# Attention blocks, scans and output stores given out later in a hybrid two-layer encoder, weight splits put first, one copy moved into the unit before

## The chip, the cores and the metric

The kernel runs on one core of a Trainium2 chip. The metric is the device time of one execution in microseconds; the median of three runs of the kernel before is 2544.51 us. The core has TensorE (PE in the profile, its weight loads apart as PEld), VectorE (DVE), ScalarE (ACT), GpSimd (POOL) and SyncE (SP, which here only issues DMAs). Each engine takes its own instructions in the order of the program and waits on semaphores for the others.

## The reference

Two layers run over 640 tokens: 512 of a prompt and 8 times 16 of a decode batch with 512 cached keys each. A layer computes, in float32:

```
h = rms_norm(x);  z = h @ w_in            # u, v | q, k, v, indexer | q, k, v | three gates
oa = u * (block-causal W_s @ rms_norm(gelu(v)) + bias)              # branch a
ob = softmax attention, 8 query heads on 2 kv heads, keys chosen by
     the top 128 (132) of an indexer's relu scores                   # branch b
oc = stick-breaking attention, 8 heads: w = exp(log_sigmoid(z) + suffix sum of log_sigmoid(-z))
x += (sum of sigmoid(gate_i) * (o_i @ w_br_i)) @ w_out
x += (silu(g) * up) @ w_ffn_out
x += sigmoid(rms_norm(x) @ w_ple_gate) * (p @ w_ple_proj)
```

The new keys and values of both attentions, the indexer keys and the normalised v rows are outputs as well.

## The kernel before

The 640 tokens lie on the free axis as two halves of 320 (`HN`), the 1024 model columns as 8 tiles of 128 partitions. All projections are fp32 work done as three single-pass products: weights and activations are split into a high and a low part, and `rows` (three matmuls of 320 columns for each k tile, PSUM tile `pd`) sums high x high, low x high and high x low. `token_tiles` does the same with tokens as the stationary side (`pn`). Attention uses the names `cz`, `czs` (branch c logits, prompt and decode), `bl`, `bls` (branch b), `ix`, `ixs`, `is` (indexer), `tpw` (transposes of the weights of a block), `av`, `avs`, `avb` (weights times values), `hcs`, `sp` (sums for the head norms and their spread).

Weights come in chunks of at most 128x1024 in a fixed order (`CHUNKS`). `load_chunk` issues the DMA into one of two `raw` tiles, copies it into one of three `hi` tiles on ACT (L219) and subtracts on DVE, or on POOL for the chunks 18 to 36 of a layer, into one of three `lo` tiles (L220). A layer is a list of units in the order of the string `ORDER`, then the merges of the branches, the output projection, the feed-forward part and the last gate. The units named cq, ck (branch c queries, keys), bq, bk, av, au and ga are projections of one 128-column tile each, 48 matmuls, 7 us.

Attention is written as Python generators that are put between the projection matmuls. `add` queues a task in one of two lists (`sc` for branch c, `si` for the indexer and branch b) with a due time `self.T + START`; `mm` advances the clock `T` by an assumed price for each matmul; `pump`, called every six matmuls or so, runs every task that is due up to its next `yield`, whose value is the time to wait (a multiple of `LAG`). `logits_room` holds the one double PSUM tile `qk` of the logits for a given time, `room` the two `tp` tiles. `until` runs tasks to their end before a unit that needs them. After that a scheduler settles each engine's own order from these priorities.

The pieces that the change and the prediction touch are these. `stick_prompt` (branch c, one block of 128 queries) makes the logits, adds the mask on DVE (L952), takes a sigmoid on ACT (L955), scans on DVE (L942), subtracts (L959) and hands over to `av_prompt`, which transposes, multiplies by the values, copies to the tile `ots` (L937) and stores it (L938). `dsa_prompt` is the same for branch b, with the softmax in lines 1032 to 1040. `stack_q` makes the split query tiles `qs` (copy on ACT L549, subtraction on POOL L550), `stack_k` the key tiles `ks` and `kl` (L560 to L563). `u_bk` projects branch b's keys; `key_norm`, called in the following unit bq0, spreads their norm with a POOL copy `hrb` (L616) and ten matmuls `sp`. `head_rms` makes `hcs`, for which ACT first squares the tile (`hsq`, L607).

Of the kernel before, what the change touches and what calls it, by code (L numbers as in the profile page):

```python
# [9 lines left out]
F32 = mybir.dt.float32  # L10
F32R = mybir.dt.float32r
BF = mybir.dt.bfloat16
U32 = mybir.dt.uint32
AF = mybir.ActivationFunctionType
OP = mybir.AluOpType
# [43 lines left out]
def _chunk(w, ks, cols):  # L59
# [4 lines left out]
ORDER = ("cq0 ck0 av0 cq1 av1 ck1 cq2 au0 au1 ck2 cq3 au2 ck3 au3 "  # L64
         "bk0 bq0 ga0 ga1 bq1 ga2 bq2 ga3 ga4 bq3 ga5 ga6 ga7")

# [78 lines left out]

ND, NQ, NTP = 4, 1, 2
LAG, LOAD1, LOAD4, START = 1.2, 3.5, 8.0, 2.5
PAIRED = (("c", 0), ("c", 1), ("c", 2), ("c", 3), ("b", 0), ("b", 1), ("b", 2), ("b", 3), "bs")
# [22 lines left out]
class Net:  # L171
    def __init__(self, tc, A, cst, big, wp, wk, sm, ps):
        nc = tc.nc
        self.tc, self.nc, self.A = tc, nc, A
        self.cst, self.big, self.wp, self.wk, self.sm, self.ps = cst, big, wp, wk, sm, ps
        self.con = con = cst.tile([128, C_N], F32, name="con")
        self.ident = con[:, C_ID:C_ID + 128]
        self.cmask = con[:, C_CM:C_CM + 128]
        self.adm = con[:, C_ADM:C_ADM + 128]
        self.gcol = []  # L180
        for l in range(L):
            g = cst.tile([128, G_N], F32, name=f"gcol{l}")
            (nc.gpsimd if l else nc.sync).dma_start(g, A["cols"][l])
            self.gcol.append(g)
        self.ones = cst.tile([128, 1], F32, name="ones")
        nc.vector.memset(self.ones, 1.0)
        self.zero = cst.tile([128, 1], F32, name="zero")
        nc.vector.memset(self.zero, 0.0)
        self.half = cst.tile([128, 16], F32, name="half")
        nc.vector.memset(self.half, -0.5)  # L190
        self.T, self.qk_free, self.tp_due = 0.0, 0.0, [0.0, 0.0]
        self.n_loaded = 0
        self.ready = []
        self.later = []
        self.x = big.tile([128, KD, NT], F32, tag="m20", name="x0")
        self.load_chunk(3, lambda k: nc.sync.dma_start(self.x[:, k], A["xT"][:, k]))
        nc.sync.dma_start(con, A["con"])
        for k in range(3, KD):
            if k in (3, 6):
                self.load_chunk()  # L200
            nc.sync.dma_start(self.x[:, k], A["xT"][:, k])


    def load_chunk(self, pieces=1, also=None):
        nc, i = self.nc, self.n_loaded
        self.n_loaded += 1
        w = CHW[i % NCH] // pieces
        raw = self.wp.tile([128, 1024], F32, tag="raw", name=f"raw{i}", bufs=2)
        hi = self.wp.tile([128, 1024], F32R, tag="hi", name=f"hi{i}")
        lo = self.wp.tile([128, 1024], F32R, tag="lo", name=f"lo{i}")  # L210
        low = nc.gpsimd if LO_POOL[0] <= i % NCH < LO_POOL[1] else nc.vector
        for p in range(pieces):
            c = slice(w * p, w * p + w)
            nc.sync.dma_start(raw[:, c], self.A["w"][i // NCH, i % NCH, :, c])
            if also:
                also(p)

            def split(c=c):
                nc.scalar.activation(hi[:, c], raw[:, c], AF.Copy)  # L219
                low.tensor_tensor(lo[:, c], raw[:, c], hi[:, c].bitcast(F32), op=OP.subtract)  # L220

            if p:
                self.later.append(split)
            else:
                split()
        self.ready.append((hi, lo))
# [56 lines left out]
    def tp(self, name):  # L283
        self.tp_due = [self.tp_due[1], self.T + 1.0]
        return self.ps.tile([128, 512], F32, tag="tp", name=name, bufs=NTP)
# [97 lines left out]
    def batch_rows(self, b):  # L383
        t = self.at.tile([128, 8, 16], BF, tag="es", name="es", bufs=1)
        nc, con = self.nc, self.con
# [4 lines left out]
    def pump(self):  # L390

        if self.busy:
            return
        self.busy = True
        for q in (self.sc, self.si):
# [10 lines left out]
    def step(self, q, t):  # L406
# [9 lines left out]
        t.past |= t.held  # L416
        t.due = self.T + (wait[0] if t.held else wait)

    def until(self, q, *names):
# [181 lines left out]
    def u_bk(self, j, ch):  # L601
        nc, S = self.nc, self.S
# [6 lines left out]
        self.head_rms(sq, r, 64)  # L609
        S["bkz"], S["rk"] = z, r  # L610

    def key_norm(self):
        nc, S, l, gl = self.nc, self.S, self.l, self.gl
        z, r = S["bkz"], S["rk"]
        rb = self.wk.tile([128, 5, 2, 64], F32, tag="t2", name="hrb", bufs=1)
        nc.gpsimd.tensor_copy(rb.rearrange("p t s d -> p (t s) d"),  # L616
                              r.rearrange("p t s -> p (t s)")[:, :, None].to_broadcast([128, 10, 64]))
        b0, b1 = self.spread(lambda t: rb[:, t].rearrange("p s d -> p (s d)"))
# [39 lines left out]
    def reload(self, br):  # L658

        src = []  # L660
        for j in range(4):
            if br == "a":
                t = self.S["au"][:, j]
# [130 lines left out]
    def index_prompt(self):  # L794
# [17 lines left out]
        for i in range(1, 4):  # L812
# [14 lines left out]
            for hp in range(4):  # L827
                yield from self.logits_room(LAG * (0.4 + 1.7e-3 * n))
                qk = self.qk2("ix")
# [19 lines left out]
        iws = self.at.tile([128, 2, 128], F32, tag="iws", name="iws", bufs=1)  # L849
        ia = self.at.tile([128, 8, 16], F32, tag="osb", name="iwa", bufs=1)  # L850
        nc.vector.tensor_tensor(ia, iw[:, 4][:, :, None].to_broadcast([128, 8, 16]),
# [18 lines left out]
    def index_sample(self):  # L870
# [5 lines left out]
        for b in range(NB):  # L876
            nc.gpsimd.tensor_copy(kx[:, PAST:], ikr[:, 16 * b:16 * b + 16])
            yield 0.4
            yield from self.logits_room(LAG * 0.9)
            qk = self.qk2("ixs")  # L880
# [12 lines left out]
            else:  # L893
                yield LAG * 0.9
                for hf in range(2):
                    p = self.tp("is")
# [28 lines left out]
    def av_prompt(self, w, vt, o, j, i, m):  # L925
# [4 lines left out]
        yield from self.room(1)  # L930
        ot = self.at.tile([128, 128], F32, tag="os" + m, name="ots", bufs=1)
        av = self.tp("av")
# [4 lines left out]
        nc.vector.tensor_copy(ot, av[:, :128])  # L937
        nc.sync.dma_start(o[:, j, 128 * i:128 * i + 128], ot)  # L938

# [4 lines left out]
    def stick_prompt(self, j, i, q, k, vt):  # L944
# [14 lines left out]
        nc.vector.tensor_tensor(g[:, :, :n], g[:, :, 1:n + 1], g[:, :, :n], op=OP.subtract)  # L959
        yield (LAG * (0.6 + 6.6e-3 * n),)  # L960
        yield from self.av_prompt(g, vt, self.A["s_oc"][self.l], j, i, "c")

    def stick_sample(self):
# [7 lines left out]
        for b in range(NB):  # L971
# [4 lines left out]
            yield 0.6  # L976
            yield from self.logits_room(LAG * 1.2)
            qk = self.qk2("czs")
# [24 lines left out]
            if b < NB - 1:  # L1003
                kc = [self.past("kc", self.A["c_k"][l, b + 1, :, j]) for j in range(4)]
                loaded = self.T + LOAD4
            at = self.at.tile([128, 128], F32, tag="osc", name="at", bufs=1)
            nc.scalar.activation(at, av[:, :128], AF.Copy)
# [13 lines left out]
    def dsa_prompt(self, j, i, q):  # L1021
        nc, S = self.nc, self.S
        vt, k, rq = S["bvp"], S["bk"], S["rq"]
        n = 128 * (i + 1)
        yield from self.logits_room(LAG * (0.4 + 4.2e-3 * n))
        qk = self.qk2("bl")
# [17 lines left out]
    def dsa_sample(self):  # L1044
# [10 lines left out]
        def first():  # L1055
            ra = self.at.tile([128, 2, 4, 16], F32, tag="osb", name="ra", bufs=1)
            for s in range(2):
# [150 lines left out]
```

## Time and profile before

| what | us |
|---|---|
| median of three runs | 2544.51 |
| lowest, highest | 2542.89, 2545.09 |
| the profiled execution's own time | 2545.36 |
| its span from the first to the last instruction | 2543.6 |
| TensorE busy in the span | 2469.8 (97%) |
| weight loads busy | 2347.1 (92%) |
| DVE, ACT, POOL busy | 1356.2 (53%), 940.9 (37%), 316.8 (12%) |

The busy time of an engine is the time in which one of its instructions runs; matmuls are pipelined, so one that starts every 0.147 us is shown with 0.31 us. PEclk is the clock that TensorE was granted as a share of full speed. Windows are given in us from the start of the span. A wait row names the instruction that waited, what it waited for, the us in total, the number of times and the longest. Layer one runs up to about 1270, layer two after it; attention lies in the first 500 us of each.

### The profile page before, as it was taken

The page shows a single profiled execution, that of the slowest core. Times are in us where ns is not written, and L with a number is a line of the kernel's source. Part 1 is how long each engine was busy: PE and PEld are TensorE (multiplying, and loading weights), DVE is VectorE, ACT ScalarE, POOL GpSimd, SP SyncE. Part 2 cuts the span into 40 slices and gives each one's busy share as a digit, 9 for nine tenths or more (in the row PEclk, how much of TensorE's full clock was granted, in tenths as well). Part 3 has the DMA queues.
Part 4 walks back from the last instruction along what each step waited for, and adds up shares of the span by engine and source line. Part 5 has one row for each costly group of instructions (what it writes and reads, how often), then busy time and mean ns, then how long its engine had stood idle before and what let it go on. Part 6 is the DMA issues. An engine that isn't in the chain of part 4 may idle for free.

```text
span 2543.6 us, 42312 instructions
## 1 busy us (share of the span) xinstructions
PE 2469.8 (97%) x17528; PEld 2347.1 (92%) x17528; DVE 1356.2 (53%) x2447; ACT 940.9 (37%) x1365; POOL 316.8 (12%) x375
## 2 busy tenths in 40 slices
PE   8989999999999999999999998999999999999999
PEld 8887778899999999999998877788999999999999
DVE  5885754554544334345558948446445443343454
ACT  4644554532332122123346345556223321221231
POOL 1122322100001000000011223221000000010100
PEclk9999999999999999999999999999999999999999
DMA  5222244532422222222342221445323222222222
GB/s 192 86 68 85 73 128 143 157 105 75 133 69 75 75 75 76 76 74 78 101 142 87 72 82 65 140 130 178 99 75 127 69 81 76 75 74 77 69 81 75
DMA packets 102399, 242.89 MB, mean 95 GB/s; under 512 B 11152, under 2 KB 33952, under 8 KB 102208
## 3 DMA queue, kind: packets, MB, share of 16 engines
q1 hardware_dynamic: 99552, 229.81, 29.1%
q0 software_dynamic: 2656, 10.38, 1.1%
q8 instruction: 138, 2.26, 0.4%
q14 instruction: 53, 0.43, 0.1%
HBM read 221.07 MB, written 19.08 MB: 94 GB/s over the span
## 4 chain that ended last, share of the span: by engine, by line
PE 84%; DVE 8%; issue 3%; ACT 2%; POOL 2%; DMA 1%; SPq 0%; DVEq 0%; POOLq 0%; ACTq 0%
PE pd L273 71%; PE pn L273 4%; DVE cg L942 2%; PE tpw L281 2%; PE av L273 1%; DVE m L788 1%; DVE sc L791 1%; PE bl L273 1%; POOL qs L550 1%; PE czs L273 1%; ACT hi L219 1%; PE ixs L273 1%; PE bls L273 1%; DVE cg L959 1%; PE is L273 1%
## 5 line engine op out<-in xcount | busy, mean ns | idle before, releaser
L219 ACT ACTIVATE hi<-raw 128x1024 fp32r<-128x1024 f32 (+4 forms) x306 | 316.5, 1034 | 1114.1 <-PE pd L273 656.4
L273 PE MATMUL pd<-fh,lo 128*128 128x320 f32 x1664 | 513.5, 309 | 0.0
L273 PE MATMUL pd<-fh,hi 128*128 128x320 f32 x1664 | 513.4, 309 | 0.0
L273 PE MATMUL pd<-fl,hi 128*128 128x320 f32 x1664 | 513.1, 308 | 0.0
L273 PE MATMUL pd<-xh,hi 128*128 128x320 f32 x1568 | 498.4, 319 | 0.0
L273 PE MATMUL pd<-xh,lo 128*128 128x320 f32 x1568 | 492.1, 314 | 2.4 <-DVE lo L220 2.4
L273 PE MATMUL pd<-xl,hi 128*128 128x320 f32 x1568 | 493.9, 315 | 0.0
L220 DVE TENSOR_TENSOR lo<-raw,hi 128x1024 fp32r<-128x1024 f32 (+4 forms) x268 | 368.1, 1373 | 143.6 <-ACT hi L219 143.0
L273 PEld LDWEIGHTS pd<-xh,hi 128*128 128x128 f32 x1568 | 298.0, 190 | 17.9 <-issue 16.8
L273 PEld LDWEIGHTS pd<-fh,hi 128*128 128x128 f32 x1664 | 312.3, 188 | 0.1
L273 PEld LDWEIGHTS pd<-fh,lo 128*128 128x128 f32 x1664 | 312.3, 188 | 0.0
L273 PEld LDWEIGHTS pd<-fl,hi 128*128 128x128 f32 x1664 | 312.3, 188 | 0.0
L273 PE MATMUL pd<-mid,hi 128*128 128x320 f32 x1408 | 309.9, 308 | 0.0
L273 PEld LDWEIGHTS pd<-xh,lo 128*128 128x128 f32 x1568 | 299.1, 191 | 9.6 <-issue 6.5
L273 PEld LDWEIGHTS pd<-xl,hi 128*128 128x128 f32 x1568 | 299.0, 191 | 4.8 <-issue 4.3
L273 PEld LDWEIGHTS pd<-mid,hi 128*128 128x128 f32 x1408 | 235.5, 188 | 0.0
L273 PE MATMUL pd<-mid,lo 128*128 128x320 f32 x704 | 217.0, 308 | 0.0
L749 POOL TENSOR_TENSOR fu<-fu,fg 128x640 f32<-128x640 f32 x44 | 68.9, 1566 | 772.3 <-DVE fu L337 772.3
L730 DVE TENSOR_TENSOR x<-x,pd 128x320 f32<-128x320 f32 x128 | 61.7, 486 | 193.4 <-PE pd L273 191.6
L337 DVE TENSOR_TENSOR fu<-pd,rs 128x320 f32<-128x320 f32 x88 | 43.3, 492 | 191.9 <-PE pd L273 191.9
L273 PEld LDWEIGHTS pd<-mid,lo 128*128 128x128 f32 x704 | 132.1, 188 | 0.0
L337 DVE TENSOR_TENSOR gt<-pd,rs 128x320 f32<-128x320 f32 x96 | 46.9, 490 | 156.7 <-PE pd L273 156.6
(264 smaller groups left out, 3765.5 us busy)
## 6 DMA issues: line engine op xcount, KB each, us to landing
raw<-w SPq DMA_DIRECT2D x270, 512.0 KB, 3.6
kc<-c_k SPq DMA_DIRECT2D x64, 256.0 KB, 5.3
kc<-c_v SPq DMA_DIRECT2D x64, 256.0 KB, 3.7
raw<-w SPq DMA_DIRECT2D x16, 384.0 KB, 3.1
raw<-w SPq DMA_DIRECT2D x11, 468.0 KB, 4.2
ka<-b_k SPq DMA_DIRECT2D x16, 256.0 KB, 2.8
kv<-b_v SPq DMA_DIRECT2D x16, 256.0 KB, 3.0
x<-xT SPq DMA_DIRECT2D x8, 320.0 KB, 5.8
```

What stands on the lines that cost most here:

```text
L219: nc.scalar.activation(hi[:, c], raw[:, c], AF.Copy)
L220: low.tensor_tensor(lo[:, c], raw[:, c], hi[:, c].bitcast(F32), op=OP.subtract)
L273: self.nc.tensor.matmul(out, a, b, start=start, stop=stop)
L281: self.nc.tensor.transpose(out, src, self.ident)
L337: self.nc.vector.tensor_tensor(dst[:, sl], pt[h][:, :HN], self.rs[:, sl], op=OP.mult)
L550: nc.gpsimd.tensor_tensor(q[b, s], z[a, :NP], q[a, s].bitcast(F32), op=OP.subtract)
L730: self.nc.vector.tensor_tensor(x[:, c, sl], x[:, c, sl], pt[h][:, :HN], op=OP.add)
L749: nc.gpsimd.tensor_tensor(u, u, g, op=OP.mult)
L788: nc.vector.max(out=m8, in_=sc[:, :n])
L791: nc.vector.match_replace(out=sc[:, :n], in_to_replace=m8, in_values=sc[:, :n], imm_value=TAKEN)
L942: self.nc.vector.tensor_tensor_scan(r, r, self.zero.to_broadcast([128, n]), 1.0, op0=OP.mult, op1=OP.add)
L959: nc.vector.tensor_tensor(g[:, :, :n], g[:, :, 1:n + 1], g[:, :, :n], op=OP.subtract)
```

## The change

`ORDER` moves the unit bq1 to directly behind bq0 and the later ones of branch b one place earlier. New attention tasks become due 6.0 instead of 2.5 after they are queued (`START`). The waits between the scan and the transposes of a branch c block, and the holds of the logits tile, are longer by 0.5 to 1.0 times `LAG`; a `tp` tile counts as taken for 1.5 instead of 1.0, and the indexer's `is` step now asks for both. The store of `ots` is issued 2.0 later, through a list that `pump` empties (`soon`, `catch_up`). The small tiles `ots`, `at`, `iwa`, `ra` and `es`, each alone or in pairs under a tag with one buffer, share the tag `os` with three. The two instructions of a weight split are traced with a priority raised by 200. The copy `hrb` moves from `key_norm` (unit bq0) to the end of `u_bk`. No instruction of TensorE, DVE or POOL is added or removed; ACT has four table loads fewer in the program.

```
-         "bk0 bq0 ga0 ga1 bq1 ga2 bq2 ga3 ga4 bq3 ga5 ga6 ga7")
+         "bk0 bq0 bq1 ga0 ga1 bq2 ga2 ga3 bq3 ga4 ga5 ga6 ga7")
...
-ND, NQ, NTP = 4, 1, 2
-LAG, LOAD1, LOAD4, START = 1.2, 3.5, 8.0, 2.5
+ND, NQ, NTP, OS = 4, 1, 2, 3
+LAG, LOAD1, LOAD4, START = 1.2, 3.5, 8.0, 6.0
...
-                nc.scalar.activation(hi[:, c], raw[:, c], AF.Copy)
-                low.tensor_tensor(lo[:, c], raw[:, c], hi[:, c].bitcast(F32), op=OP.subtract)
+                with self.tc.high_priority(offset=200):
+                    nc.scalar.activation(hi[:, c], raw[:, c], AF.Copy)
+                    low.tensor_tensor(lo[:, c], raw[:, c], hi[:, c].bitcast(F32), op=OP.subtract)
...
-        self.tp_due = [self.tp_due[1], self.T + 1.0]
+        self.tp_due = [self.tp_due[1], self.T + 1.5]
...
+    def soon(self, delay, f):
+        self.todo.append((self.T + delay, f))
+    def catch_up(self, all=False):
+        while self.todo and (all or self.todo[0][0] <= self.T):
+            self.todo.pop(0)[1]()
...
+        rb = self.wk.tile([128, 5, 2, 64], F32, tag="t2", name="hrb", bufs=1)
+        nc.gpsimd.tensor_copy(rb.rearrange("p t s d -> p (t s) d"),
+                              r.rearrange("p t s -> p (t s)")[:, :, None].to_broadcast([128, 10, 64]))
+        S["bkz"], S["rkb"] = z, rb
...
-        ot = self.at.tile([128, 128], F32, tag="os" + m, name="ots", bufs=1)
+        ot = self.at.tile([128, 128], F32, tag="os", name="ots", bufs=OS)
...
-        nc.sync.dma_start(o[:, j, 128 * i:128 * i + 128], ot)
+        self.soon(2.0, lambda: nc.sync.dma_start(o[:, j, 128 * i:128 * i + 128], ot))
...
-        yield (LAG * (0.6 + 6.6e-3 * n),)
+        yield (LAG * (1.6 + 6.6e-3 * n),)
...
-        yield from self.logits_room(LAG * (0.4 + 4.2e-3 * n))
+        yield from self.logits_room(LAG * (1.2 + 4.2e-3 * n))
```

The first place is TensorE behind the unit bq3 of layer one, where the logits `bl` of that unit's first block are made from `qs`. Before:

```order
L273 MATMUL avs<-kc,wT 32x128 [waits DMAHW1_49]
L273 MATMUL avs<-kc,wT 32x128 x3
L273 MATMUL bl<-ks,qs 128x256 [waits Pool_49]
L273 MATMUL bl<-kl,qs 128x256
L273 MATMUL pd<-xh,hi_4194 128x320
L273 MATMUL bl<-ks,qs 128x256 [waits Pool_49]
L273 MATMUL bl<-kl,qs 128x256
```

In the changed program the same logits stand in one piece:

```order
L274 MATMUL avs<-kc,wT 32x128 [waits DMAHW0_49]
L274 MATMUL avs<-kc,wT 32x128 x3
L274 MATMUL bl<-ks,qs 128x256 [waits Pool_49]
L274 MATMUL bl<-kl,qs 128x256
L274 MATMUL bl<-ks,qs 128x256 [waits Pool_49]
L274 MATMUL bl<-kl,qs 128x256
L274 MATMUL pd<-xh,hi_3932 128x320
```

Between the last matmul of bq3 and the first of these rows stand 12 projection matmuls in the order before and 36 in the changed one.

The second place is ACT in layer one, where branch c's first key tiles `ks` and `kl` are made beside the indexer's `ixr` and the weight split of the next chunk (`hi_950` before, `hi_929` now). Before:

```order
L833 ACTIVATE ixr<-ix 128x2x384 [waits PE_49,Pool_49]
L833 ACTIVATE ixr<-ix 128x2x384 [waits DVE_49,PE_49,Activation_49] x2
L219 ACTIVATE hi_950<-raw_949 128x1024 [waits DMAHW2_49,PE_49]
L560 ACTIVATE ks<-ckz 64x512 [waits DVE_49]
L561 ACTIVATE ks<-ckz 64x512
```

Now:

```order
L220 ACTIVATE hi_929<-raw_928 128x1024 [waits DMAHW2_49,PE_49,Activation_49]
L570 ACTIVATE ks<-ckz 64x512 [waits DVE_49]
L571 ACTIVATE ks<-ckz 64x512
L570 ACTIVATE ks<-ckz 64x512
L571 ACTIVATE ks<-ckz 64x512
L844 ACTIVATE ixr<-ix 128x2x384 [waits PE_49,Pool_49]
L573 ACTIVATE kl<-kl 64x512 [waits DVE_49] x2
```

The split and the key tiles moved ahead of the indexer's steps.

The third place is POOL around the norm of the keys (`rk` the norm, `hrb` its copy, `cgs` a column that is set to one). Before:

```order
L598 TENSOR_TENSOR rk<-hr,half 128x10 [waits DVE_49]
L987 MEMSET cgs 128x1 [waits PE_49,Pool_49]
L616 COPY hrb<-rk 128x640 [waits Pool_49]
L550 TENSOR_TENSOR qs<-bqz,qs 64x512 [waits Activation_49,Pool_49]
L550 TENSOR_TENSOR qs<-bqz,qs 64x512 [waits Activation_49]
```

Now:

```order
L608 TENSOR_TENSOR rk<-hr,half 128x10 [waits DVE_49]
L621 COPY hrb<-rk 128x640 [waits PE_49,DMAHW4_49,Activation_49,Pool_49]
L999 MEMSET cgs 128x1 [waits PE_49]
L999 MEMSET cgs 128x1 [waits DVE_49,PE_49]
L221 TENSOR_TENSOR lo_2959<-raw_2957,hi_2958 128x1024 [waits DMAHW2_49,PE_49,Activation_49]
```

On POOL the copy only passed one memset; on TensorE the matmuls `hcs` that lead to it moved from behind the last matmul of bq0 to its 16th, while `sp`, which reads it, stands at the end of bq0.

## Rows read from the trace of the kernel before

**Rows 1.** Windows by stage: us, busy time (and count) of PE, PEld, DVE, ACT, POOL, PEclk, DMA share, GB/s.
```profile
30.00:515.00 485.00, 454.13 (x3406) 394.97 (x3404) 318.87 (x720) 254.64 (x423) 106.72 (x133) 0.98 0.35 108
515.00:1300.00 785.00, 784.68 (x5400) 781.71 (x5399) 360.91 (x507) 218.72 (x263) 54.77 (x59) 1.00 0.28 88
1300.00:1790.00 490.00, 459.95 (x3475) 401.46 (x3473) 323.51 (x733) 257.47 (x427) 104.95 (x131) 0.98 0.34 107
```

**Rows 2.** Waits of PE, 30 to 515 us: total, times, longest.
```profile
PE bl L273 <- POOL qs L550: 7.2, 4, 2.8
PE tpw L281 <- DVE cg L959: 5.9, 6, 2.0
PE cz L273 <- issue: 3.8, 1, 3.8
PE cz L273 <- ACT ixsr L889: 2.5, 2, 1.5
PE cz L273 <- ACT kl L563: 1.7, 2, 1.2
PE pd L273 <- DVE lo L220: 1.2, 1, 1.2
PE sp L273 <- POOL hrb L616: 1.2, 1, 1.2
PE is L273 <- DVE ots L937: 1.1, 1, 1.1
```

**Rows 3.** Timeline of PE behind bq3: start, duration, [idle before <-releaser].
```profile
435.23 1.28 PE L273 MATMUL hcs<-con,hsq 128*128 128x2 f32 x10
...
440.86 0.58 PE L273 MATMUL bl<-ks,qs 128*128 128x256 f32 x1 [2.75 <-POOL qs L550]
```

**Rows 4.** Timeline of POOL there.
```profile
435.83 1.32 POOL L550 TENSOR_TENSOR qs<-bqz,qs 64x512 fp32r<-64x512 f32 x1 [2.94 <-ACT qs L549]
437.23 1.96 POOL L598 TENSOR_TENSOR rq<-hr,half 128x10 f32<-128x10 f32 x1
...
439.55 1.26 POOL L550 TENSOR_TENSOR qs<-bqz,qs 64x512 fp32r<-64x512 f32 x1
```

**Rows 5.** Timeline of DVE behind the unit ck1.
```profile
146.67 0.49 DVE L342 SCALAR_TENSOR_TENSOR ckz<-pd,rs 128x320 f32<-128x320 f32 x1
...
149.26 4.51 DVE L498 SCALAR_TENSOR_TENSOR va<-va,rv,vgain 128x512 f32<-128x512 f32 x5
...
154.29 0.33 DVE L342 SCALAR_TENSOR_TENSOR ckz<-pd,rs 128x192 f32<-128x192 f32 x1
```

**Rows 6.** Timeline of PE at the first logits that need those keys.
```profile
156.04 0.55 PE L273 MATMUL cz<-ks,qs 128*128 128x256 f32 x1 [3.79 <-issue]
```

**Rows 7.** Windows: a stretch at the lower clock, and one at the full clock.
```profile
439.20:446.00 6.80, 5.14 (x21) 5.15 (x22) 1.86 (x9) 0.91 (x5) 1.85 (x5) 0.50 0.58 199
600.00:606.80 6.80, 6.80 (x49) 6.80 (x48) 4.36 (x7) 1.78 (x2) 0.00 (x0) 1.00 0.20 57
```

**Rows 8.** Timeline of PE at a pair of transposes between projection matmuls.
```profile
100.20 0.28 PE L273 MATMUL pn<-hi,xh 128*128 128x256 f32 x1
100.41 0.44 PE L281 MATMUL tpw<-con,cg 128*128 128x128 f32 x2
100.61 0.37 PE L273 MATMUL pn<-hi,xl 128*128 128x256 f32 x1
100.81 0.28 PE L273 MATMUL pn<-lo,xh 128*128 128x256 f32 x1
100.93 0.28 PE L273 MATMUL pn<-hi,xh 128*128 128x256 f32 x1
```

**Rows 9.** The copy `hrb`: count, then ns min/median/max, first and last start.
```profile
L616 POOL COPY hrb<-rk x2: 715/715/715, 294.4 to 1558.7; 128x640 f32<-128x640 f32 x2
```

**Rows 10.** Timeline of ACT at the squares of branch b's keys.
```profile
288.22 0.74 ACT L607 ACTIVATE hsq<-bkz 128x640 f32<-128x640 f32 x1 [6.63 <-DVE bkz L337]
```

**Rows 11.** Groups by line, 30 to 515 us: busy us, mean ns, idle before and releasers.
```profile
L219 ACT ACTIVATE hi<-raw 128x1024 fp32r<-128x1024 f32 (+2 forms) x42 | 43.5, 1036 | 48.0 <-PE pd L273 20.0 <-issue 16.2 <-DMA raw<-w 8.2
```

**Rows 12.** Waits of SP's queue, 30 to 515 us.
```profile
SPq L938 <- DVE ots L937: 104.1, 21, 12.0
```

More of the change, by code (lines that the diff above doesn't have):

```diff
@@ L190, in __init__ @@
         nc.vector.memset(self.half, -0.5)
-        self.T, self.qk_free, self.tp_due = 0.0, 0.0, [0.0, 0.0]
+        self.T, self.qk_free, self.tp_due, self.todo = 0.0, 0.0, [0.0, 0.0], []
         self.n_loaded = 0
@@ L383, in batch_rows @@
     def batch_rows(self, b):
-        t = self.at.tile([128, 8, 16], BF, tag="es", name="es", bufs=1)
+        t = self.at.tile([128, 8, 16], BF, tag="os", name="es", bufs=OS)
         nc, con = self.nc, self.con
@@ L393, in pump @@
             return
+        self.catch_up()
         self.busy = True
@@ L609, in u_bk @@
         self.head_rms(sq, r, 64)
[L610 to L614, printed above, removed]
         rb = self.wk.tile([128, 5, 2, 64], F32, tag="t2", name="hrb", bufs=1)
@@ L617, in key_norm @@
                               r.rearrange("p t s -> p (t s)")[:, :, None].to_broadcast([128, 10, 64]))
+        S["bkz"], S["rkb"] = z, rb
+    def key_norm(self):
+        nc, S, l, gl = self.nc, self.S, self.l, self.gl
+        z, rb = S["bkz"], S["rkb"]
         b0, b1 = self.spread(lambda t: rb[:, t].rearrange("p s d -> p (s d)"))
@@ L660, in reload @@
         src = []
+        self.catch_up(True)
         for j in range(4):
@@ L827, in index_prompt @@
             for hp in range(4):
-                yield from self.logits_room(LAG * (0.4 + 1.7e-3 * n))
+                yield from self.logits_room(LAG * (0.9 + 1.7e-3 * n))
                 qk = self.qk2("ix")
@@ L849, in index_prompt @@
         iws = self.at.tile([128, 2, 128], F32, tag="iws", name="iws", bufs=1)
-        ia = self.at.tile([128, 8, 16], F32, tag="osb", name="iwa", bufs=1)
+        ia = self.at.tile([128, 8, 16], F32, tag="os", name="iwa", bufs=OS)
         nc.vector.tensor_tensor(ia, iw[:, 4][:, :, None].to_broadcast([128, 8, 16]),
@@ L878, in index_sample @@
             yield 0.4
-            yield from self.logits_room(LAG * 0.9)
+            yield from self.logits_room(LAG * 1.9)
             qk = self.qk2("ixs")
@@ L894, in index_sample @@
                 yield LAG * 0.9
+                yield from self.room(2)
                 for hf in range(2):
@@ L976, in stick_sample @@
             yield 0.6
-            yield from self.logits_room(LAG * 1.2)
+            yield from self.logits_room(LAG * 2.0)
             qk = self.qk2("czs")
@@ L1005, in stick_sample @@
                 loaded = self.T + LOAD4
-            at = self.at.tile([128, 128], F32, tag="osc", name="at", bufs=1)
+            at = self.at.tile([128, 128], F32, tag="os", name="at", bufs=OS)
             nc.scalar.activation(at, av[:, :128], AF.Copy)
@@ L1055, in first @@
         def first():
-            ra = self.at.tile([128, 2, 4, 16], F32, tag="osb", name="ra", bufs=1)
+            ra = self.at.tile([128, 2, 4, 16], F32, tag="os", name="ra", bufs=OS)
             for s in range(2):
```

## The prediction

> **What bounds the kernel now.** I read the windows by stage first. The reader is to see that TensorE has hardly an idle moment outside the two stretches with attention: 785.00 - 784.68 = 0.3 us between 515 and 1300, against 485.00 - 454.13 = 30.9 us from 30 to 515 and 490.00 - 459.95 = 30.1 us from 1300 to 1790 [rows 1]. The change touches only these stretches, and it adds or removes no matmul. So there are some 61 us of idle time to win, plus what the clock does there: PEclk is 0.98 in both and 1.00 between them.
>
> The waits of TensorE come second. Eight rows name 24.6 of the 30.9 us of layer one, and all eight are attention or a weight split that comes too late for a matmul already at the head of the queue [rows 2]. None is a weight DMA. Layer two repeats the pattern with nearly the same idle time, so I work out one layer and double it.
>
> The Trainium skill (page "Perfetto Trace Analysis", section "Identifying the Most-Contended Engine") says that busy time of matmuls is a poor measure of the distance to the roofline and that the busy share of weight loads is a better one. By that, the first stretch has 485.00 - 394.97 = 90 us of headroom rather than 31 [rows 1]. I do not take it into the sum, since transposes and attention matmuls of other shapes fill part of the difference and are all still there.
>
> **The change part by part, per layer.** For each wait I compare how much TensorE work stands between the producer and the waiting matmul in the two orders. A projection matmul starts every 6.80 / 49 = 0.139 us in the plain stretch [rows 7]; the logits, transposes and values between come on top.
>
> *Logits of branch b behind `qs`: 7.2 us in four waits [rows 2].* The worst is that of bq3: both `qs` subtractions with the norm `rq` between them end at 439.55 + 1.26 = 440.81, and the second pair of logits starts at 440.86 after 2.75 us of idle [rows 3, 4]. Before, 12 projection matmuls stand ahead of these logits behind bq3, now 36. The 24 more are worth 24 x 0.139 = 3.3 us, more than the 2.75 that was waited. Behind bq1 there are now some 160 matmuls, since the logits of bq0 come first; behind bq2 54 instead of 15; behind bq0 73 instead of 36. POOL's queue still holds `rq` between the two `qs`, which is why I leave 0.5. Gain 6.7.
>
> *Transposes of branch c behind `cg`: 5.9 us in six waits of at most 2.0 [rows 2].* The extra LAG is 1.2 us of the program's own clock for every block. The orders show what came of it: from the logits of the blocks with 512 keys to their first transposes there were 45 projection matmuls in the second head pair and are now 87, and in the third 30 and now 42. Two short blocks (128 keys, third pair) keep their distance. I leave 1.0. Gain 4.9.
>
> *First logits of a head pair: 3.8 + 2.5 + 1.7 = 8.0 us [rows 2].* The 2.5 and 1.7 go: behind ck0 the first logits stand after 45 matmuls instead of 24, behind ck2 after some 80 instead of 30, behind ck3 only the indexer's `is` and a dozen `ixs` are added, about 2 us against the 1.7 that the wait there had. The 3.8 is another thing. DVE runs the five `va` products (4.51 us) between the two halves of `ckz`; the second half is done at 154.29 + 0.33, and the logits follow at 156.04 [rows 5, 6]. The changed order has the five products at the same place; only 42 matmuls instead of 35 stand ahead of the logits, 1.0 us, but DVE has the indexer's `max` steps later and can begin the products about 2 us sooner. All four logits now stand together, so they also wait for `kl`. I keep 2.0 of the 8.0. Gain 6.0.
>
> *The copy, the stores and the splits: 1.2 + 1.1 + 1.2 = 3.5 us.* The copy `hrb` takes 0.715 us [rows 9]; it is done as soon as the norm is, while 32 matmuls of bq0 still run (4.4 us), so its wait of 1.2 ends. The `is` step waited for the copy to `ots`, which had one buffer for each branch and now shares three. The store costs SP nothing that TensorE sees: SP stood 104.1 us behind `ots` at these stores while no weight DMA was waited for [rows 12, 2], so issuing them 2.0 later only lets loads pass. POOL's write of `es` may now wait for a store three `os` tiles back, and behind it on POOL stand the `kc` copies; the tile before had one buffer and waited for a matmul, so I bound this between a gain and a loss of 1 us and take zero. The late `lo` of the first projection unit stays behind `max` steps on DVE; I leave half of it. Gain 2.6.
>
> *A new wait.* `hcs` of branch b's keys stands 16 matmuls behind the unit bk instead of 49, 2.2 us. It needs DVE's second half of `bkz` and 0.74 us of ACT; before, ACT idled 6.63 us for that half [rows 10]. In the changed DVE order it stands ahead of the two scans of 512 keys rather than behind them, but behind one `max` and the split of branch a. Bounds: nothing if DVE is up to date, 6.6 if it is as late as before. I take 2.0, near the lower end because the scans are behind it now. Queued behind `hcs` is all of bq0.
>
> *The rest* of the 30.9, 6.3 us, I leave as it is: the decode part, whose distances hardly differ. Longer holds of `qk` cost nothing as long as tasks are done before the merge that needs them; the last values of branch b stand at about the same place (2103 projection matmuls into the layer, 2118 before).
>
> Sum of the waits: 6.7 + 4.9 + 6.0 + 2.6 - 2.0 = 18.2 us, 36.4 for both layers.
>
> *The clock.* PEclk of 0.98 over 485 us is 485 x 0.02 / 0.5 = 19.4 us at the lower of the two levels, 1.2 instead of 2.4 GHz. In 6.80 us at that level TensorE began 21 matmuls against 49 [rows 7]; part of that is the wait ahead of them, and I put the loss at 0.4 of the time, 7.8 us per layer. These stretches begin right behind the long waits: this one starts inside the idle time that ends at 440.86 [rows 3, 7]. I let the loss fall in the share of the waits, 18.2 / 30.9, so by 4.6, 9.2 for both. The bounds are nothing and 15.6.
>
> The Trainium skill ("TensorE: Matmul & The Clock Gate", Part 1) says that the slow clock is the default state and that activity releases it. The trace agrees as far as it goes, with 1.00 between 515 and 1300 where nothing idles [rows 1]; by the rule alone the whole loss could go, which is a rival below.
>
> *Fewer interruptions.* The stream of projection matmuls is broken 343 times instead of 367. Around a pair of transposes the steps are 0.21 and 0.20 us where 0.12 is the plain step [rows 8], so a break costs 0.17 and 24 of them 4.1 us. This part can be nothing if the other breaks become dearer.
>
> Together: 2545.4 - 36.4 - 9.2 - 4.1 = 2495.7, so 2496. It starts from the profiled execution's own time, 2545.36, which is 1.8 above its span and 0.9 above the median; I take nothing off for that.
>
> **Rivals.**
>
> *The waits move (chance 0.24).* DVE is 66% busy in the first stretch [rows 1], and everything that is given out later meets other work there: the scans now run beside the projections' evacuations of later units. Each lost distance costs at one place what it gains at another. For it speaks that orders made from assumed prices had waits all over before; against it that the distances grow nearly everywhere at once. Half of the waits and of the clock's share: 2545.4 - 18.2 - 4.6 = 2522.6.
>
> *The clock comes back whole (0.06).* If no wait is long enough to lower the clock, 15.6 instead of 9.2 is won, and with it come the shorter waits, taken as two thirds of the idle time, 40.8: 2545.4 - 40.8 - 15.6 - 4.1 = 2485; with the new `hcs` wait at nothing too, 2481.
>
> *The splits block ACT (0.08, slower).* A split needs one of three `hi` tiles back from TensorE: before, ACT idled 20.0 us in this stretch for that, at 42 splits of 1.036 us [rows 11]. If the priority puts a split ahead of an attention step that TensorE needs next, that step comes 1.04 us later plus the idle time. It decides from the point where the loss passes the 18.2 + 4.6 + 2.0 = 24.8 of a layer, that is 24 of the 42. With 30 of them it is 31.2 - 24.8 = 6.4 per layer more than before: 2558. Against it: the changed ACT order has a split directly ahead of attention in only about a dozen places, mostly where `ks` follows.
>
> *The orders hardly matter (0.05).* The waits are set by DVE's backlog alone and stay: 2545, give or take 3.
>
> **How the numbers follow.** The forecast has 0.57, with its own range 2478 to 2512. About 0.2% (5 us) is what a measurement of this kernel can tell from no change. Faster: 0.57 + 0.24 + 0.06 = 0.87; the case without effect gives 0.04 to no change and 0.01 to slower, so slower is 0.09. The range of 8 in 10 goes from 2472, where even the new wait and all the clock's loss are gone, to 2536, which holds the case of the moved waits with its own spread.
>
> **What would show it.** In the profile after, TensorE's idle time in each attention stretch should be 11 to 14 us and PEclk 0.99. The rows `bl <- qs`, `sp <- hrb` and `is <- ots` should be gone or below 0.5; `tpw <- cg` about 1; the `issue` wait of `cz` about 2; a row `hcs <- hsq` of 1 to 3 should be new at the top. The forecast is wrong if idle time stays above 22 us per layer, if `bl` still waits for POOL, or if ACT's splits appear between attention pieces that TensorE waits for.

## The result, and the profile after

| | before | after |
|---|---|---|
| median, us (4 runs each) | 2544.26 | 2501.93 |
| lowest to highest | 2542.89 to 2545.09 | 2500.76 to 2502.92 |
| profiled execution, span | 2545.36, 2543.6 | 2500.76, 2499.0 |
| time to before | | 0.9834, 95% interval 0.9817 to 0.9851 |

The change makes the kernel 42 us faster; the forecast was 2496 with a range of 2472 to 2536. The total came out well, its parts less so, and the windows by stage show it at once. The columns are those of [rows 1]; the stretches end at the same places of the program, give or take fifteen matmuls:

```profile
30.00:493.00 463.00, 439.71 (x3415) 387.93 (x3414) 319.16 (x721) 254.54 (x424) 107.42 (x132) 0.99 0.37 114
493.00:1278.00 785.00, 784.29 (x5385) 781.46 (x5384) 360.20 (x502) 217.31 (x261) 53.14 (x57) 1.00 0.28 87
1278.00:1746.00 468.00, 448.19 (x3476) 396.73 (x3475) 324.48 (x735) 251.07 (x422) 107.33 (x132) 0.98 0.36 111
```

All of the gain lies in the two stretches with attention; the long one between them is unchanged. TensorE's idle time there was 30.87 + 30.05 = 60.9 us [rows 1] and is 23.29 + 19.81 = 43.1: 17.8 less, where I had forecast 36.4. Its busy time fell by 914.1 - 887.9 = 26.2 us for ten matmuls more, where I had forecast 13.3 (clock and interruptions).

The waits of TensorE in the first stretch, as in [rows 2]:

```profile
PE tpw L282 <- DVE cg L971: 3.9, 4, 2.9
PE tpw L282 <- DVE hr L607: 3.0, 2, 1.7
PE cz L274 <- ACT kl L573: 2.4, 2, 1.6
PE hcs L274 <- ACT hsq L660: 2.2, 1, 2.2
PE ix L274 <- ACT ixr L844: 1.9, 2, 1.4
PE bls L274 <- DMA ka<-b_k: 1.5, 2, 1.3
PE cz L274 <- ACT cg L967: 1.4, 2, 1.0
PE iwT L282 <- DVE iwa L862: 1.2, 1, 1.2
PE pd L274 <- DVE lo L221: 1.2, 1, 1.2
...
PE pd L274 <- ACT ohc L277: 0.8, 1, 0.8
```

`bl <- qs`, once 7.2, is gone, and so are `sp <- hrb`, `is <- ots` and the `issue` wait of `cz`. In their place stand waits that are new or longer: `tpw <- hr`, `hcs <- hsq`, `ix <- ixr`, `iwT <- iwa`. In this stretch `tpw <- cg` has fewer waits but one that is longer than any before, 2.9 against 2.0.

That one is worth following. The timeline of TensorE, and below it those of POOL and DVE (the same columns as in [rows 3]):

```profile
165.12 0.44 PE L282 MATMUL tpw<-con,cg 128*128 128x128 f32 x2 [2.88 <-DVE cg L971]
```
```profile
159.69 2.42 POOL L221 TENSOR_TENSOR lo<-raw,hi 128x1024 fp32r<-128x1024 f32 x1 [7.14 <-ACT hi L220]
162.18 2.60 POOL L560 TENSOR_TENSOR qs<-cqz,qs 64x512 fp32r<-64x512 f32 x2
```
```profile
160.13 2.25 DVE L954 TENSOR_TENSOR_SCAN cg<-cg,zero 128x128 f32<-128x128 f32 x1
162.30 0.66 DVE L799 MAX8 m<-sc 128x8 f32<-128x512 f32 x1
162.89 0.83 DVE L954 TENSOR_TENSOR_SCAN cg<-cg,zero 128x128 f32<-128x128 f32 x1
163.65 0.06 DVE L802 MATCH_VALUE_LOAD sc<-m,sc 128x8 f32 x1
163.70 0.67 DVE L802 MATCH_REPLACE8 sc<-m,sc 128x512 f32<-128x512 f32 x1
164.29 0.78 DVE L971 TENSOR_TENSOR cg<-cg 128x256 f32<-128x256 f32 x1
```

A scan of 128 keys takes 0.42 us at the median of its sixteen; here the first takes 2.25. It began 0.44 after POOL's subtraction for a weight split began and ended 0.27 after that one ended. The second scan (0.83) and the difference in L971 (0.78 against 0.43) run beside POOL's next two subtractions, those for `qs`. The wait `tpw <- hr` has the same history. DVE there, POOL beside it, and TensorE behind:

```profile
267.11 4.46 DVE L954 TENSOR_TENSOR_SCAN cg<-cg,zero 128x512 f32<-128x512 f32 x2
271.50 0.06 DVE L802 MATCH_VALUE_LOAD scs<-m,scs 128x8 f32 x1
271.55 0.69 DVE L802 MATCH_REPLACE8 scs<-m,scs 128x528 f32<-128x528 f32 x1
272.16 0.15 DVE L607 TENSOR_SCALAR hr<-hcs 128x10 f32<-128x10 f32 x1
```
```profile
268.10 2.39 POOL L221 TENSOR_TENSOR lo<-raw,hi 128x1024 fp32r<-128x1024 f32 x1 [9.65 <-ACT hi L220]
```
```profile
268.72 1.26 PE L274 MATMUL hcs<-con,hsq 128*128 128x2 f32 x10
...
272.36 0.55 PE L282 MATMUL tpw<-con,cg 128*128 128x128 f32 x3 [1.72 <-DVE hr L607]
```

The sums of squares of the keys, `hcs`, waited for nothing themselves. But `hcs` holds one of the two `tp` tiles until DVE has read it as `hr`, and `hr` stands behind two scans, the second of which took 3.32 us instead of 1.22. The transposes wait for the tile.

### The profile page after: what moved, and what is told of

The parts are those of the page before. It is cut to its first block, busy times and chain, and to the rows that moved or that the text cites. A ratio compares the mean times of both kernels' runs of the same rounds, so it can differ in the third digit from the quotient of the medians.

```text
span 2499.0 us, 42360 instructions
## 1 busy us (share of the span) xinstructions
PE 2443.1 (98%) x17528; PEld 2335.2 (93%) x17528; DVE 1357.0 (54%) x2447; ACT 935.5 (37%) x1361; POOL 317.6 (13%) x375
```

## Experiments: one part undone at a time

Four kernels on one chip, each the changed one with one part as before. The kernel before, timed beside each group of four experiments, took 2545.57, 2542.97 and 2542.71 us in the three groups, so a difference between times of different groups, the changed kernel's among them, is good to some 3 us. A ratio is always to the kernel before of the same group.

```
-LAG, LOAD1, LOAD4, START = 1.2, 3.5, 8.0, 6.0
+LAG, LOAD1, LOAD4, START = 1.2, 3.5, 8.0, 2.5
```


> The changed kernel with START back at 2.5. Theory A (added distance removes the waits, and START gives most of it): the waits of bl for POOL's qs, 15.1 us over both layers before and none after, come back nearly whole, and of the first logits cz the 8.0 us that were won; with two to four stretches at the lower clock (1.7 us each) that is +20 to +27, so 2522 to 2529. Theory B (the other parts, the order of units and the LAG terms, already give the distance): within 5 of 2502.

Measured 2521.38, ratio to before 0.9902 (0.9889 to 0.9916): 19.5 more than the changed kernel, just under theory A's range. Two waits came back where it says, here over both layers:

```profile
PE cz L274 <- issue: 7.6, 2, 3.8
PE bl L274 <- POOL qs L560: 6.6, 4, 3.0
PE tpw L282 <- DVE hr L607: 5.8, 4, 1.7
```

The first row is as large as before. The second is not half of it (15.1 before), where theory A had it nearly whole: the order and the holds give some distance too, and with one of them undone this wait is 2.9 or 3.5 (the next two runs). The third row is no return; it is 5.9 in the changed kernel.

```
-         "bk0 bq0 bq1 ga0 ga1 bq2 ga2 ga3 bq3 ga4 ga5 ga6 ga7")
+         "bk0 bq0 ga0 ga1 bq1 ga2 bq2 ga3 ga4 bq3 ga5 ga6 ga7")
```


> The changed kernel with the old ORDER. Theory A: the logits of each branch b unit keep their distance by START alone, some 25 matmuls, so at most 2 us a layer return: 2502 to 2508. Theory B (bq1 directly behind bq0 is what spreads branch b's work): bl waits again for qs and the last avb is late, 2512 to 2520.

Measured 2504.83, ratio 0.9838 (0.9824 to 0.9851): not to be told from the changed kernel. `bl <- qs` is back with 2.9, `hcs <- hsq` is gone, and 3.4 of the 5.9 us of `tpw <- hr` are left. Theory B falls.

```
-        yield (LAG * (1.6 + 6.6e-3 * n),)
+        yield (LAG * (0.6 + 6.6e-3 * n),)
...
-                yield from self.room(2)
```


> The changed kernel with every LAG term, the tp time and the second room of the is step as before. Theory A: the waits of tpw for cg were 10.8 us before and are 8.2 after, so this part is worth 3 to 6 with the is step: 2505 to 2508, the rows tpw<-cg and is at the top of the waits. Theory B (the longer holds of the logits tile are what keeps blocks apart): 2515 or more. Theory C (the holds only delay, and the delays cause the new waits of ix, ohc and ka): faster, 2495 to 2499.

(The other LAG terms and the `tp` time went back too.) Measured 2507.80 (2502.62 to 2510.50), ratio 0.9847 (0.9831 to 0.9862): the median is in theory A's range, the interval holds no effect as well. `tpw <- cg` was not worse, 4.7 us against 8.2 with the LAG terms, so the longer waits ahead of the transposes did not buy what I had put on them.

```
-                with self.tc.high_priority(offset=200):
+                if True:
```


> The changed kernel with the weight splits at their old priority. Theory A: TensorE waited only 1.2 us for lo and 0.4 for hi per layer, before and after, so 2500 to 2504. Theory B (the splits' priority frees ACT and DVE for nothing else and delays attention steps such as kl, cg, hr, which are the waits left): faster, 2492 to 2498. Theory C (it is what kept the new order from starving the projections): 2508 or more.

Measured 2496.35, ratio 0.9808 (0.9793 to 0.9823): 5.6 less. No help from the priority shows; `cz <- kl` falls from 5.0 to 3.1 over both layers and `tpw <- cg` from 8.2 to 5.4 without it. The rival "the splits block ACT" had this sign and was far too big. The intervals touch, so the size is uncertain.

## Experiments: the tiles, the copy, and POOL's subtractions

```
-        ot = self.at.tile([128, 128], F32, tag="os", name="ots", bufs=OS)
+        ot = self.at.tile([128, 128], F32, tag="os" + m, name="ots", bufs=1)
...
-        self.soon(2.0, lambda: nc.sync.dma_start(o[:, j, 128 * i:128 * i + 128], ot))
+        nc.sync.dma_start(o[:, j, 128 * i:128 * i + 128], ot)
```


> The changed kernel with the small tiles in their old tags and the stores issued at once. Theory A: only the wait of is for the copy to ots (2.2 us in both layers before) comes back, SP's earlier stores cost nothing: 2502 to 2506. Theory B (the four parts undone one at a time so far add up to 23 of the 43 us, and what is missing sits here: one buffer for a tile makes DVE wait at the copy for the store, and the queue behind it): 2512 to 2520, with DVE waiting for a DMA at ots.

(All five tiles went back to their tags.) Measured 2512.35, ratio 0.9880 (0.9866 to 0.9893): 10.4 more, in theory B's range. B's mechanism is there: DVE waits for the store at `ots` four times, 4.7 us over both layers, where the changed kernel shows no such wait. TensorE does not wait longer for `ots` itself. The one of its waits that grew much is `tpw <- cgs`, in the decode part, from 1.7 to 5.7 over both layers; and the trace's clock records show 34.1 us at the lower clock in the two stretches instead of 23.9. How the 10 us divide is not shown.

The copy `hrb` back in `key_norm`, first alone:

```
+        S["bkz"], S["rk"] = z, r
+
+    def key_norm(self):
...
-        S["bkz"], S["rkb"] = z, rb
-
-    def key_norm(self):
```


> The changed kernel with the copy hrb back in key_norm. Theory A: the matmuls hcs stand 16 matmuls behind bk with and without this part, so the new waits of tpw for hr (5.9 us) and of hcs for hsq (4.4 us) stay and only sp <- hrb can return: 2502 to 2505. Theory B (moving the copy brought those waits): 2492 to 2497 and the two rows gone.

Measured 2501.31, ratio 0.9838 (0.9824 to 0.9851): no effect. And with the priority taken out as well:

> The changed kernel without the splits' priority and with the copy hrb back. Theory A: as without the priority alone (2496) plus at most the 2.3 us of sp <- hrb: 2495 to 2499. Theory B: the copy's place costs several us of its own: 2488 to 2492.

Measured 2498.15, ratio 0.9825 (0.9812 to 0.9838). So the copy's move neither won the 2.3 us of its wait nor brought the new ones.

The last kernel of this group takes up the long scans, on top of the version without priority:

```
-LO_POOL = (18, 37)
+LO_POOL = (99, 99)
```


> The changed kernel without the splits' priority and with every subtraction of a weight split on DVE, none on POOL. In the trace after, a scan of 512 keys that began while POOL subtracted took 3.32 us against 1.22, one of 128 keys 2.25 against 0.41. Theory A (DVE operations of two SBUF operands stand still while POOL's subtraction of 2.4 us runs, so a split on POOL costs DVE up to 2.1 us where one on DVE costs 1.37): no scan longer than 1.3 us, the waits tpw <- hr 1.7 and tpw <- cg 2.9 shorter, 2486 to 2495. Theory B (the long scans are late operands or chance, and DVE, 69% busy here, gets 19 splits of 1.37 us more per layer): the waits grow, 2500 to 2515.

Measured 2467.35, ratio 0.9703 (0.9690 to 0.9716): 29 us below the version without priority (27 by the ratios) and 35 below the changed kernel, more than theory A dared. The same place on DVE, and the windows:

```profile
260.69 2.34 DVE L954 TENSOR_TENSOR_SCAN cg<-cg,zero 128x512 f32<-128x512 f32 x2
262.95 0.07 DVE L802 MATCH_VALUE_LOAD scs<-m,scs 128x8 f32 x1
263.00 0.69 DVE L802 MATCH_REPLACE8 scs<-m,scs 128x528 f32<-128x528 f32 x1
263.61 0.16 DVE L607 TENSOR_SCALAR hr<-hcs 128x10 f32<-128x10 f32 x1
```
```profile
30.00:463.00 433.00, 422.60 (x3312) 374.32 (x3312) 312.84 (x723) 246.51 (x411) 64.31 (x113) 1.00 0.37 115
463.00:1248.00 785.00, 783.74 (x5401) 779.73 (x5398) 364.68 (x515) 220.50 (x265) 50.14 (x49) 1.00 0.28 89
1248.00:1700.00 452.00, 443.10 (x3463) 392.15 (x3463) 321.79 (x742) 252.62 (x425) 66.80 (x123) 1.00 0.37 117
```

The two scans take 2.34 instead of 4.46, idle time is 10.4 and 8.9 us, and the clock is 1.00 throughout. (The first stretch ends 103 matmuls, some 15 us, earlier in the program than the changed kernel's, so its length cannot be set against that one; the idle times can.) Of the waits of the version without priority, `tpw <- hr` (5.9 us over both layers) and `cz <- kl` (3.1) are gone, and `hcs <- hsq` falls from 4.4 to 1.2. No wait of TensorE for POOL stood in that version's list, so a POOL that is free earlier could explain the gain only by way of another engine. The busy times on the two pages price it, first of the changed kernel, then of this one:

```profile
PE 2443.1 (98%) x17528; PEld 2335.2 (93%) x17528; DVE 1357.0 (54%) x2447; ACT 935.5 (37%) x1361; POOL 317.6 (13%) x375
```
```profile
PE 2431.9 (99%) x17528; PEld 2325.5 (94%) x17528; DVE 1360.2 (55%) x2485; ACT 937.0 (38%) x1361; POOL 230.9 (9%) x337
```

DVE does 38 subtractions more, and the time of all its subtractions in this trace is 51.6 us longer (366.8 to 418.4), but it is busy only 3.2 us longer. All its other instructions, added one by one over the trace, are 39.9 us shorter (1082.5 to 1042.6). So the same subtractions on POOL had cost DVE some 40 us of standing still by this sum, up to 48 by the busy time, in which back-to-back instructions overlap a little.

## Experiments: is it one cause or two

With START standing out and a second cause found, three kernels were to set them apart, and a fourth to try for more.

The kernel before with `LO_POOL = (99, 99)` and nothing else:

> The kernel before with every subtraction of a weight split on DVE, none on POOL, and nothing else changed. Theory A (what made the waits of before was mostly DVE standing still during POOL's subtractions; the added distance of the change covers that up): the gain is as large here as in the changed kernel, 29 us or more, 2505 to 2516, and little is left for the distance. Theory B (distance and standstill are two causes that add up): the waits of bl for POOL's qs and the first logits behind the five va products stay, so 15 to 25 are won: 2520 to 2530, and the changed order is worth some 50 on top.

Measured 2506.88, ratio 0.9856 (0.9841 to 0.9871). The gain of 35.8 us is as large as theory A says, but its conclusion, that little is left for the distance, is wrong: the change without its priority takes the time from 2506.88 to 2467.35, by 39.5 us, where it wins some 48 by itself. The causes add up but for a fifth, nearly as theory B says, and this one is bigger than B had it. `bl <- qs` is still there:

```profile
PE bl L273 <- POOL qs L550: 11.9, 6, 2.8
PE czs L273 <- DVE st L1032: 8.0, 2, 4.0
PE tpw L281 <- DVE cg L959: 6.4, 9, 1.9
```

The changed kernel with the store at once but the shared tag:

> The changed kernel with the stores of ots issued at once, the shared tag of three buffers kept. It parts the 10 us of tags and stores together. Theory A (as forecast: the time of the store costs SP nothing that TensorE sees; the 10 us are the tags): 2500 to 2504. Theory B (a store that waits at the head of SP's queue holds the weight and key loads behind it): 2507 to 2512.

Measured 2502.62, ratio 0.9840 (0.9825 to 0.9855): no effect. With three shared buffers the time of the store is worth nothing, so the 10 us need the old tags. The old tags with the later store were not run.

START = 6.0 alone:

> The order of before in everything but START, which is 6.0 (the helper for later stores is present and unused). Theory A (the parts add up; START undone cost 19.5): 2522 to 2527. Theory B (later starts need the three small buffers and the longer holds to pay, or they pile up): 2530 to 2540. Theory C (START takes most of what any of the parts could win): 2508 to 2516.

Measured 2510.05, ratio 0.9872 (0.9856 to 0.9887), 32.7 below before: theory C. The other parts together give the remaining 10 and, without START, 24. The windows of this kernel say why it does so well (about the same stretches, each a little longer):

```profile
30.00:500.00 470.00, 449.29 (x3423) 393.19 (x3423) 321.60 (x723) 256.87 (x424) 105.74 (x131) 0.99 0.36 111
1285.00:1765.00 480.00, 460.46 (x3550) 403.09 (x3549) 329.64 (x742) 258.47 (x427) 105.54 (x131) 1.00 0.35 110
```

Idle time, 20.7 and 19.5 us, is already less than in the full change, and the clock records show 10.2 us at the lower clock against 23.9.

Last, the version with all subtractions on DVE, and the two scans and the difference of a block put ahead of the indexer's steps by a priority of 60:

```
-        for s in range(2):
-            self.suffix_product(g[:, s], n)
...
+        with self.tc.high_priority(offset=60):
+            for s in range(2):
+                self.suffix_product(g[:, s], n)
...
```


> The changed kernel without the splits' priority, all subtractions on DVE, and the two scans and the difference of a branch c block traced with a priority raised by 60, so that they stand ahead of the indexer's max steps. Theory A (tpw <- cg, 5.1 us, is the largest wait left and comes from max steps put between the scans): that row under 2 us, 2461 to 2465. Theory B (a branch c block put ahead makes the other chains late by as much): 2466 to 2472.

Measured 2467.89, ratio 0.9704 (0.9688 to 0.9719): no gain. `tpw <- cg` went from 5.1 only to 4.5. The version before it stays the best, and beats both kernels.

## Why the prediction came out right, and where its steps failed

*Right as a total, and partly by luck.* The profiled execution fell by 44.6 us; I had 49.7. The waits were to give 36.4 and gave 17.8 by the idle time; clock and interruptions were to give 13.3 and the busy time gave 26.2. Two misses of opposite sign. By the prediction's own sign of being wrong, idle time above 22 us in a layer, its account of the waits fails in layer one (23.3) and just passes in layer two (19.8); 11 to 14 had been forecast. Two slips in the working are small beside this: the parts of "the copy, the stores and the splits" add up to 2.9 and not 2.6, and a plain projection matmul starts every 0.147 us, not every 0.139.

*`bl <- qs`: right.* 6.7 forecast, 7.2 won in layer one, and START holds much of it: with START back, 6.6 of the 15.1 us of both layers return.

*First logits: right in kind.* 8.0 us became 2.4 + 1.4 = 3.8, where I had left 2.0. The `issue` wait is gone rather than halved, and the four logits that now stand together wait for `kl`, as foreseen.

*`hrb`, `ots`, `lo`: right for the first two rows, wrong for the third.* `sp <- hrb` and `is <- ots` went, but undoing the copy's move changed no time. `lo` kept its whole 1.2, where I had it halved.

*`tpw <- cg`: wrong.* I left 1.0 a layer; 3.9 and 4.3 us remained. The step counted distance on TensorE and took the duration of the work on DVE as given. It was not: in the timeline above the two scans and the difference run from 160.13 to 165.07, and their 2.25 + 0.83 + 0.78 us stand against 0.42 + 0.42 + 0.43 at the median, 2.6 us more beside POOL's work; indexer steps of 1.4 us lie between. In the version with the splits on DVE and without priority no wait of this kind is above 1.3 us. In the kernel before with the splits on DVE one of 1.9 is left; there the distance is missing.

*The new wait: the place was right, the mechanism half.* 2.0 was forecast at `hcs` of the keys. What came is 3.0 for the `tp` tile that these sums hold, and 2.2 at the sums of bq0 (the sums of bk had waited 0.6 for theirs before, [rows 2] does not list it). It did not come from the copy: with the copy put back both waits are what they were, 5.9 and 4.4 us over both layers. The 2.2 came from the order; with the old one it is gone, but 3.4 us of the wait for the `tp` tile stay.

*The waits that move: I gave this rival 0.24, and for the waits it is what happened:* half of the forecast. `ix`, `bls`, `iwT` and `ohc`, 5.4 us in layer one, stood in no term of mine.

*The clock: right in size, not in its rule.* 9.2 us were forecast. The clock records show 44.4 us at the lower level in the two stretches before and 23.9 after; at the 0.4 of the prediction that is 8.2. The 0.4 is fair: inside such records of the kernel before a projection matmul starts every 0.27 us and outside every 0.147, so a busy microsecond loses 0.45. But I let the loss fall by the share of the waits that go, and by that share the 17.8 us won would have given 4.6. START alone shows that the sum of the idle time does not set it: 40.2 us of idle time, nearly as much as the full change's 43.1, and only 10.2 us at the lower level. The version with all subtractions on DVE has none there, with 19.3 us of idle time.

*Interruptions: mis-sized, and the count is not their measure.* 4.1 us were forecast, from 24 breaks fewer; 26.2 - 8.2 = 18 is what the fall in busy time leaves for all steps that are not idle time. A matmul that starts every 0.147 us is shown with 0.31, so a wait below some 0.16 is inside the busy time, and part of the 18 may be such waits. The runs show which parts of the change it goes with. START alone lowers TensorE's busy time by 15.1 us (2469.8 to 2454.7), and its 34.2 us less at the lower clock make 13.7 of them at 0.4, so hardly any of the 18 is START's. With the LAG terms undone the busy time is 11.5 us longer than in the changed kernel (2454.6 against 2443.1) at the same 23.9 us of lower clock, although the traces count 336 breaks of the projections' stream there and 343 in the changed kernel. So much of it goes with the longer waits and holds. What in them saves the time stays open.

*The stores: right.* SP's wait behind `ots` fell from 104.1 [rows 12] to 54.0, and issuing them at once again cost nothing. *The shared tags: missed.* I gave them the 1.1 us of `is <- ots` and bounded the rest by one microsecond; undone together with the stores they are worth some 10.

## What to carry to other kernels

Before you count how much work stands between a producer and a wait, look at the longest and the median duration of the producer's own instructions: [rows 2] named DVE's `cg`, and one look at that line's minimum, median and maximum (0.40, 0.93 and 2.83 us, where the longest shape takes 1.21 at its own median) would have shown scans two to three times too long. An instruction that is given to an idle engine is free only if that engine takes nothing from the one that is waited for: here 38 subtractions on POOL cost DVE 40 us or more, where doing them itself took 51.6. And it matters only where somebody waits for that engine: in the feed-forward part of the best version 44 products on POOL (`fu`) stretch DVE's subtractions by some 48 us in all, and TensorE idles for hardly more than 1 us in layer one's part of it (785.00 - 783.74 in the window above). Of an order change with many parts, the one that moves everything may hold most of the gain: START alone won 32.7 of the 42 us.

## What the runs showed of the hardware that was not expected

POOL and DVE exclude each other for some operations. It stood in the trace before, too, beyond the rows that I had read. The second scan of 384 keys of one block, beside POOL's subtraction:

```profile
171.81 0.94 DVE L942 TENSOR_TENSOR_SCAN cg<-cg,zero 128x384 f32<-128x384 f32 x1
173.31 2.83 DVE L942 TENSOR_TENSOR_SCAN cg<-cg,zero 128x384 f32<-128x384 f32 x1
```
```profile
172.91 2.42 POOL L220 TENSOR_TENSOR lo<-raw,hi 128x1024 fp32r<-128x1024 f32 x1 [1.92 <-ACT hi L219]
```

POOL is done at 175.33; 0.94 on top of that is 176.27, and the scan ends at 176.14. In the kernel before with the splits on DVE the same scan, with no POOL beside it, takes its usual time:

```profile
171.66 0.95 DVE L942 TENSOR_TENSOR_SCAN cg<-cg,zero 128x384 f32<-128x384 f32 x1
```

Other DVE operations run through such a subtraction undisturbed. In the changed kernel POOL subtracts from 170.31 to 172.83, and DVE beside it shows

```profile
170.58 0.68 DVE L802 MATCH_REPLACE8 sc<-m,sc 128x512 f32<-128x512 f32 x1
171.18 0.42 DVE L964 TENSOR_TENSOR cz<-cz,con 128x256 f32<-128x256 f32 x1
171.51 0.68 DVE L799 MAX8 m<-sc 128x8 f32<-128x512 f32 x1
172.11 0.47 DVE L338 TENSOR_TENSOR va<-pd,rs 128x320 f32<-128x320 f32 x1
```

all at their usual length. The two that add or multiply here take one operand from PSUM (`cz`, `pd`). All 28 MAX8 and MATCH_REPLACE8 steps that meet such a subtraction in this trace keep theirs. Two inputs from SBUF are not the only case, though: the step `bqbd <- bqz` (TENSOR_SCALAR in L657, one tile and a column of factors) takes 0.25 us at the least and 2.39 at the most, beside POOL.

The Trainium skill ("SBUF — State Buffer", section "SBUF: two separate sides") says that DVE and GpSimd share one pair of ports as an exclusive lock, which a DVE operation needs when it has two inputs in SBUF or runs in a mode that uses both ports, and that the later one blocks for the other's whole instruction. The traces agree for the scans, which read two tiles in SBUF and stood still until POOL's end, and for the four operations above, which did not; whether `bqbd` ran in such a mode no row shows. The other way round is there as well: in the kernel before a subtraction on POOL that began with 0.57 us left of a DVE product of two SBUF tiles (`va <- gmt,va`) took 2.80 instead of 2.39. By that rule the price of a subtraction on POOL is up to its 2.4 us on DVE; on average it was 40 / 38 to 48 / 38, that is 1.1 to 1.3, here.
